# Hymba trunk in float32: the FFN's gate and up projections as seven block products with weight sums on GpSimd

## The chip, the core and the metric

The kernel runs on one core of a Trainium2 chip. TensorE (PE) multiplies matrices into PSUM, VectorE (DVE) and ScalarE (ACT) do elementwise work, GpSimd (POOL) does slow elementwise work, masks and some DMA issues, SyncE (SP) issues most of the DMAs. Each engine runs its own instructions in order and waits on semaphores of the others. The metric is the device time of one launch in microseconds (us), as a median over runs.

## What is computed

Two layers of a decoder trunk over 544 tokens (one prompt of 512, eight samples of 4), all in float32, model width 1024. Each layer is a half-step FFN, a mixer (gated DeltaNet heads and sliding-window attention), and a second half-step FFN; a norm ends the trunk. Four FFNs in all, each with a hidden width of 2816. What matters here:

```python
def _swiglu(x, w_gate, w_up, w_down):
    return (jax.nn.silu(x @ w_gate) * (x @ w_up)) @ w_down

def _layer(x, conv_buf, gdn_s, k_buf, v_buf, p):
    x = x + 0.5 * _swiglu(_rmsnorm(x, n1), g1, u1, d1)
    h = _rmsnorm(x, nm) @ w_in
    ...
    x = x + jnp.concatenate([gdn_o, swa_o], axis=-1) @ w_out
    x = x + 0.5 * _swiglu(_rmsnorm(x, n2), g2, u2, d2)
```

## The kernel before, in words

Activations are feature-major: `x` is eight tiles of 128 features by 544 tokens. A float32 product is made of three passes of a faster format (fp32r): every operand is split into a high part and a low part (what the high part leaves), and high by high, high by low and low by high are added up in PSUM. So a weight tile of 128 output columns by 1024 inputs costs 8 x 3 matmuls for each of two token halves (`HALVES`, 256 and 288 columns wide), 48 in all. The matmul is in `mm3` (L539), and `project` runs both halves.

A weight tile comes by a DMA of SP into one of three `raw` buffers. `split_w` makes `whi` on ACT (L483) and `wlo` = raw - whi on DVE (L484), each of 128 partitions by 1024 elements; `next_w` and `ahead` keep up to three loads and one split ahead of the product in progress. The plan of tiles is fixed: `HID` cuts the 22 hidden tiles of an FFN into blocks of 8, 8 and 6; in a block each hidden tile has its gate product and then its up product (a *pair*), and after the block's pairs come the eight down products over that block's hidden tiles, added into `x` (L588).

A pair's results leave PSUM on DVE, multiplied by the norm's per-token factor `rb` on the way (`scaled_evac`, L559). Then `ffn` makes the hidden value: tanh on ACT (L573), two products on DVE (L574, L575), its high part on ACT (L578) and its low part on DVE (L579).

The norm before each FFN gives the high and low parts of x times the gain (`Norm.split_half`, ACT L304 and DVE L305) and sums squares (ACT L366, POOL L372, the last of eight on DVE) while the product before it is still giving out its tiles (`Norm.tile`). At the start of the program `Norm.first` and `first_sums` do this from the token-major inputs. `later` makes the mixer's constants (masks on POOL, small gate and sink loads by POOL's DMA queue, copies of cached rows by the same queue); it is called after the first block of the first FFN, and `tc.issue_after(last_pool)` asks for its work to stand behind the last POOL instruction of the first norm (`st`, L357). A scheduler places the instructions of every engine by priority and readiness, so where such work ends up is seen in the order of each engine's instructions and in the trace.

Of the kernel before, what the change touches and what calls it, by code (L numbers as in the profile page):

```python
# [24 lines left out]
HALVES = ((0, 256), (256, 288))  # L25
EPS = 1e-6
NEG = -1e30
SLOT = 571
NSLOT = 48
# [9 lines left out]
def kernel(  # L39
# [14 lines left out]
    xt_p = ctx.enter_context(tc.tile_pool(name="xt", bufs=KD))  # L54
    raw_p = ctx.enter_context(tc.tile_pool(name="raw", bufs=3))
    w_p = ctx.enter_context(tc.tile_pool(name="w", bufs=3))
# [31 lines left out]
    # ---- streams of mixer work, woven between the dense products: a stream yields 0 after  # L88
    # each product of a batch and a number of dense products to wait for after it ----
# [5 lines left out]
    def pump(steps=1):  # L95
        """let dense time pass by one product, then streams take steps"""
# [4 lines left out]
        while steps > 0:  # L101
# [53 lines left out]
    def load_par(l, rows):  # L155
        """norm gains, conv taps and output gains, one column per 128 features"""
# [4 lines left out]
        # the rms norm's sqrt(128) and the one half of silu  # L161
# [10 lines left out]
    def mixer_constants():  # L172
# [21 lines left out]
        # second half of a pair of b-blocks by its first half, and the other way round  # L194
# [12 lines left out]
        # rows of first and of second halves  # L207
# [20 lines left out]
        # rows (sample, head, step t): 1 where j <= t, for the four leading keys  # L228
# [38 lines left out]
    # scratch: one 128 x 128 matrix per (head, chunk), spaced so that all the diagonal  # L267
    # 16-blocks lie at one stride; the inverted blocks one after another
# [12 lines left out]
    x = [slot([P, NTOK], "x") for _ in range(KD)]  # L281
    xd = dram_p.tile([KD, P, NTOK], F32, name="xd")

    class Norm:
# [3 lines left out]
        def __init__(self, nw, src=None, scale=1.0 / D, n=KD):  # L288
            self.nw, self.src, self.scale, self.n = nw, src, scale, n
# [3 lines left out]
        def split(self, k, half):  # L293
            if half == 0:
                self.xh.append(xt_p.tile([P, NTOK], F32R, tag="xh", name="xh"))
                self.xl.append(xt_p.tile([P, NTOK], F32R, tag="xl", name="xl"))
# [10 lines left out]

# [1292 lines left out]
```

## Time and profile before

| | us |
|---|---|
| median of 3 runs (2368.92 to 2373.78) | 2369.38 |
| span of the profiled execution | 2358.2 |
| PE busy in it | 2312.9 |
| DVE busy | 1238.5 |
| ACT busy | 730.6 |
| POOL busy | 267.6 |

The span runs from the first to the last instruction of the profiled execution; the 11.2 us between it and the median lie around the span. Busy times are sums of the records; a matmul's record overlaps with its neighbours', so the pace of PE is read from how many matmuls pass in a stretch, not from a record's length. The program has five kinds of stretch: the start (to 80 us), the four FFNs (about 80 to 415, 800 to 1200, 1200 to 1540 and 1935 to 2350), two mixers (about 450 to 740 and 1570 to 1890), two output projections just behind them, and the final norm inside the last FFN's last products.

### The profile page before, as it was taken

How to read it: one execution, taken by the hardware profiler on the slowest of the kernel's cores; microseconds unless marked ns; L12 is line 12 of the kernel's file. 1: busy time of each engine (PE TensorE's matmuls, PEld its weight loads, DVE VectorE, ACT ScalarE, POOL GpSimd, SP SyncE). 2: the span in 40 equal slices, each digit the busy share in tenths (PEclk: the TensorE clock that was granted, in tenths of full speed). 3: DMA queues.
4: the chain of work that ended last, by engine and by line, in shares of the span. 5: the costliest groups of instructions: out<-in, count | busy, mean ns of one | idle time of the engine just before them, and what ended most of it. 6: DMA issues, size and time to landing. Idle time of an engine off the chain costs nothing.

```text
span 2358.2 us, 41922 instructions
## 1 busy us (share of the span) xinstructions
PE 2312.9 (98%) x17683; PEld 2232.4 (95%) x17683; DVE 1238.5 (53%) x2384; ACT 730.6 (31%) x1385; POOL 267.6 (11%) x359
## 2 busy tenths in 40 slices
PE   8899999999999999999999999999999999999997
PEld 7899999998988999999999999999899799999997
DVE  5444445576567553444554343456565764444344
ACT  3222223343454321222422221244235432222122
POOL 5100000233112000000100000012231220000002
PEclk9999999998999999999999999999989899999998
DMA  5623332342124323332222333243322152233222
GB/s 127 117 83 90 90 89 90 106 120 57 48 62 142 89 83 89 90 90 87 84 87 85 89 90 90 81 131 93 75 64 64 45 160 83 89 90 90 87 77 64
DMA packets 412766, 210.37 MB, mean 89 GB/s; under 512 B 39954, under 2 KB 406866, under 8 KB 412548
## 3 DMA queue, kind: packets, MB, share of 16 engines
q1 hardware_dynamic: 410504, 204.23, 30.1%
q0 software_dynamic: 992, 2.69, 1.3%
q8 instruction: 139, 2.28, 0.4%
q10 hardware_dynamic: 1084, 0.79, 0.1%
q14 instruction: 47, 0.39, 0.0%
HBM read 192.97 MB, written 16.73 MB: 89 GB/s over the span
## 4 chain that ended last, share of the span: by engine, by line
PE 92%; DVE 3%; DMA 2%; issue 1%; POOL 1%; ACT 0%; SPq 0%; POOLq 0%; DVEq 0%; ACTq 0%
PE ps_d L539 81%; PE ps_sc L1280 1%; PE ps_sp L1273 1%; DMA sink<-in_swa_sinks_dram 1%; PE ps_s L1207 1%; PE ps_Y L929 1%; PE ps_x L1108 1%; PE ps_Z L939 1%; DMA gate<-in_gdn_a_log_dram 0%; PE ps_st L1352 0%; PE ps_av L1306 0%; PE ps_ds L1069 0%; PE ps_pt L86 0%; DVE wlo L484 0%; PE ps_qk L864 0%
## 5 line engine op out<-in xcount | busy, mean ns | idle before, releaser
L539 PE MATMUL ps_d<-xh,whi 128*128 128x256 f32 (+1 forms) x3520 | 1033.1, 294 | 14.0 <-DVE sinks L261 4.9
L539 PE MATMUL ps_d<-xl,whi 128*128 128x256 f32 (+1 forms) x3520 | 1035.8, 294 | 0.0
L539 PE MATMUL ps_d<-xh,wlo 128*128 128x256 f32 (+1 forms) x3520 | 1027.4, 292 | 0.2 <-DVE wlo L484 0.2
L483 ACT CAST whi<-raw 128x1024 fp32r<-128x1024 f32 (+1 forms) x332 | 341.3, 1028 | 1187.3 <-PE ps_d L539 781.3
L539 PEld LDWEIGHTS ps_d<-xh,whi 128*128 128x128 f32 x3520 | 669.9, 190 | 20.7 <-issue 8.9
L539 PEld LDWEIGHTS ps_d<-xh,wlo 128*128 128x128 f32 x3520 | 672.3, 191 | 6.2 <-issue 3.2
L539 PEld LDWEIGHTS ps_d<-xl,whi 128*128 128x128 f32 x3520 | 670.7, 191 | 4.7 <-issue 1.1
L484 DVE TENSOR_TENSOR wlo<-raw,whi 128x1024 fp32r<-128x1024 f32 (+1 forms) x332 | 400.2, 1206 | 117.1 <-ACT whi L483 115.9
L539 PE MATMUL ps_d<-hh,wlo 128*128 128x288 f32 (+1 forms) x1408 | 405.2, 288 | 0.0
L539 PE MATMUL ps_d<-hl,whi 128*128 128x288 f32 (+1 forms) x1408 | 404.8, 288 | 0.0
L539 PE MATMUL ps_d<-hh,whi 128*128 128x288 f32 (+1 forms) x1408 | 403.0, 289 | 0.0
L539 PEld LDWEIGHTS ps_d<-hl,whi 128*128 128x128 f32 x1408 | 266.9, 190 | 0.0
L539 PEld LDWEIGHTS ps_d<-hh,wlo 128*128 128x128 f32 x1408 | 266.8, 189 | 0.0
L539 PEld LDWEIGHTS ps_d<-hh,whi 128*128 128x128 f32 x1408 | 265.6, 190 | 0.1
L372 POOL TENSOR_TENSOR sq<-sq 128x544 f32<-128x544 f32 x40 | 60.3, 1508 | 1517.4 <-DVE wlo L484 1040.1
L588 DVE SCALAR_TENSOR_TENSOR x<-ps_d,x 128x256 f32<-128x256 f32 x192 | 83.4, 440 | 254.7 <-PE ps_d L539 254.5
L559 DVE TENSOR_TENSOR g<-ps_d,rb 128x256 f32<-128x256 f32 (+1 forms) x176 | 76.8, 437 | 237.4 <-PE ps_d L539 219.2
L559 DVE TENSOR_TENSOR u<-ps_d,rb 128x256 f32<-128x256 f32 (+1 forms) x176 | 77.5, 440 | 223.3 <-PE ps_d L539 223.3
L539 PE MATMUL ps_d<-ol,whi 128*128 128x256 f32 (+1 forms) x256 | 73.8, 291 | 0.0
L539 PE MATMUL ps_d<-oh,wlo 128*128 128x288 f32 (+1 forms) x256 | 73.6, 289 | 0.0
L539 PE MATMUL ps_d<-oh,whi 128*128 128x288 f32 (+1 forms) x256 | 72.8, 291 | 0.0
L578 ACT CAST hh<-th 128x544 fp32r<-128x544 f32 x88 | 57.1, 649 | 34.3 <-DVE th L575 34.3
(399 smaller groups left out, 2080.5 us busy)
## 6 DMA issues: line engine op xcount, KB each, us to landing
raw<-in_ffn_w_gate_dram SPq DMA_DIRECT2D x88, 512.0 KB
raw<-in_ffn_w_up_dram SPq DMA_DIRECT2D x88, 512.0 KB
raw<-in_ffn_w_down_dram SPq DMA_DIRECT2D x64, 512.0 KB
raw<-in_w_in_dram SPq DMA_DIRECT2D x36, 512.0 KB
raw<-in_ffn_w_down_dram SPq DMA_DIRECT2D x32, 384.0 KB
S<-in_state_gdn_dram SPq DMA_DIRECT2D x32, 256.0 KB
xd<-x SPq DMA_DIRECT2D x16, 272.0 KB
x<-xd SPq DMA_DIRECT2D x16, 272.0 KB
```

The lines of the kernel that those rows point to most:

```text
L372: eng.tensor_tensor(out=self.sq, in0=self.sq, in1=s2, op=ALU.add)
L483: act.copy(out=hi[:, 0:kn], in_=v)
L484: dve.tensor_tensor(out=lo[:, 0:kn], in0=v, in1=hi.bitcast(F32)[:, 0:kn], op=ALU.subtract)
L539: pe.matmul(ps, a[:, k], b, start=(k == 0 and a is hi and b is rh), stop=(k == kn - 1 and a is lo))
L559: when(norm, lambda: dve.tensor_tensor(out=dst[:, o:o + n], in0=ps, in1=norm.rb[:, o:o + n], op=ALU.mult))
L578: act.copy(out=a, in_=th)
L588: dve.scalar_tensor_tensor(out=xv, in0=ps, scalar=0.25, in1=xv, op0=ALU.mult, op1=ALU.add)
L929: pe.matmul(ps[:, q], NM[q // 4][:, q % 4], T[:, q], start=True, stop=True)
L939: pe.matmul(ps[:, q], Tt[q // 4][:, q % 4], Y[:, q], start=True, stop=True)
L1108: pe.matmul(ps[:, :, r0:r0 + 4], ss[s // 4][:, s % 4], kqs[:, :, 32 * h + r0:32 * h + r0 + 4], start=True, stop=True)
L1207: pe.matmul(ps, kd[32 * h:32 * h + 32], um[i][32 * h:32 * h + 32], start=True, stop=True)
L1273: pe.matmul(ps[:, hh], sq[hh][gp, qs], kfe[gp, (n - 1) * P:n * P], start=True, stop=True)
```

## The change

**Seven products.** The two k halves (even and odd k tiles) and the two token halves of a pair's gate and up products make a 2 x 2 block product, which needs seven block products in Strassen's scheme instead of eight. One such product is over four k tiles and 272 tokens (`T0`, `T1`), 12 matmuls (`mm7`), so a pair has 84 matmuls of 272 columns where it had 96 of 256 and 288. Three weight blocks of a product are plain (b11, b21, b22), four are sums `t1`, `nt2`, `t3`, `t4`, made on POOL in `queue_pair` from the two raw tiles, 128 x 512 elements each. All seven are split (`split_part`, half tiles of 128 x 512).

**Activations.** `Norm.blocks` makes seven blocks of activations (three plain, four sums s1, ns2, s3, s4, the third on POOL) for each two k tiles, each with a high and a low part.

**Results.** `gate_up` leaves PSUM seven times: three by a copy on ACT, three by an addition to that copy on DVE, and one on DVE with the factor `rb`. The factor for the other three quarters of gate and up is now a POOL multiplication in place: half of g (272 columns), all of u (544).

**Around it.** `HID` is now 6, 6, 6 and 4; raw tiles have four buffers, half tiles of high and low parts six each, `AHEAD` is 3; a hidden value's parts (`parts`) are made in the next pair; and `later` has lost its `issue_after`.

```diff
+HT = NTOK // 2
+T0, T1 = slice(0, HT), slice(HT, NTOK)
...
+NW = 6
+AHEAD = 3
...
-    raw_p = ctx.enter_context(tc.tile_pool(name="raw", bufs=3))
-    w_p = ctx.enter_context(tc.tile_pool(name="w", bufs=3))
+    raw_p = ctx.enter_context(tc.tile_pool(name="raw", bufs=4))
+    w_p = ctx.enter_context(tc.tile_pool(name="w", bufs=NW))
...
+        def blocks(self, i):
...
+            part("a11", a[:, T0], v)
+            part("a12", b[:, T0], w)
+            act.activation(out=s1, in_=b[:, T1], func=ACTF.Copy, scale=w)
+            dve.scalar_tensor_tensor(out=s1, in0=a[:, T1], scalar=v, in1=s1, op0=ALU.mult, op1=ALU.add)
+            dve.scalar_tensor_tensor(out=ns2, in0=a[:, T0], scalar=v, in1=s1, op0=ALU.mult, op1=ALU.subtract)
+            pool.tensor_tensor(out=s3, in0=a[:, T0], in1=a[:, T1], op=ALU.subtract)
+            dve.scalar_tensor_tensor(out=s4, in0=b[:, T0], scalar=w, in1=ns2, op0=ALU.mult, op1=ALU.add)
+            part("s1", s1, None)
+            part("ns2", ns2, None)
+            part("s3", s3, v)
+            part("s4", s4, None)
+            part("a22", b[:, T1], w)
...
+        def total(n, in0, in1, op):
+            T[n] = slot([P, 4, P], "wt")
+            pool.tensor_tensor(out=T[n], in0=in0, in1=in1, op=op)
+
+        def third():
+            total("t3", b22, b12, ALU.subtract)
+            total("t4", b21, T["nt2"], ALU.add)
+            return split_part(T["nt2"])
+
+        total("t1", b12, b11, ALU.subtract)
+        total("nt2", T["t1"], b22, ALU.subtract)
...
-    HID = ((0, 8), (8, 8), (16, 6))
+    HID = ((0, 6), (6, 6), (12, 6), (18, 4))
...
+        def plus(out, ps):
+            dve.tensor_tensor(out=out, in0=ps, in1=out, op=ALU.add)
+
+        def scale(t, part):
+            pool.tensor_tensor(out=t[:, part], in0=t[:, part], in1=norm.rb[:, part], op=ALU.mult)
...
+            mm7(pb, next_half(), bk["a11"], start=True)
+            act.copy(out=g[:, T0], in_=pb)
+            mm7(pa, next_half(), bk["a12"], start=True)
+            plus(g[:, T0], pa)
+            scale(g, T0)
...
+            mm7(pb, next_half(), bk["ns2"])
+            act.copy(out=u[:, T0], in_=pb)
+            mm7(pd, next_half(), bk["s1"], start=True)
+            act.copy(out=u[:, T1], in_=pd)
+            mm7(pb, next_half(), bk["s3"])
+            plus(u[:, T1], pb)
+            mm7(pd, next_half(), bk["s4"])
+            plus(u[:, T0], pd)
+        scale(u, slice(0, NTOK))
+        mm7(pb, next_half(), bk["a22"])
+        dve.tensor_tensor(out=g[:, T1], in0=pb, in1=norm.rb[:, T1], op=ALU.mult)
...
-        with tc.issue_after(last_pool):
-            for l in range(depth):
-                par.append(load_par(l, load_par_rows(l, nc.gpsimd)))
...
+        for l in range(depth):
+            par.append(load_par(l, load_par_rows(l, nc.gpsimd)))
```

DVE in the middle of an FFN's block, one pair of before (`wlo` is a split of a whole weight tile, `g` and `u` are evacuations):

```order
L484 TENSOR_TENSOR wlo<-raw,whi 128x1024
L559 TENSOR_TENSOR u<-ps_d,rb 128x256
L574 SCALAR_TENSOR_TENSOR th<-th,g 128x544
L559 TENSOR_TENSOR u<-ps_d,rb 128x288
L575 TENSOR_TENSOR th<-th,u 128x544
L484 TENSOR_TENSOR wlo<-raw,whi 128x1024
L579 TENSOR_TENSOR hl<-th,hh 128x544
L559 TENSOR_TENSOR g<-ps_d,rb 128x256
L559 TENSOR_TENSOR g<-ps_d,rb 128x288
```

DVE at the same place of the changed kernel, 12 of the 14 rows of one pair (`wt` is a weight sum, `raw_562` the up tile of the next pair, `ps_b`, `ps_a` and `ps_d` the three PSUM tiles):

```order
L523 TENSOR_TENSOR wlo_874<-wt_781,whi_873 128x512
L708 TENSOR_TENSOR g_658<-ps_b_660,rb_420 128x272
L523 TENSOR_TENSOR wlo_891<-raw_562,whi_890 128x512
L720 SCALAR_TENSOR_TENSOR th_800<-th_800,g_658 128x544
L664 TENSOR_TENSOR g_804<-ps_a_807,g_804 128x272
L523 TENSOR_TENSOR wlo_908<-raw_562,whi_907 128x512
L721 TENSOR_TENSOR th_800<-th_800,u_659 128x544
L523 TENSOR_TENSOR wlo_930<-wt_832,whi_929 128x512
L727 TENSOR_TENSOR hl_849<-th_800,hh_848 128x544
L523 TENSOR_TENSOR wlo_956<-wt_830,whi_955 128x512
L523 TENSOR_TENSOR wlo_973<-wt_925,whi_972 128x512
L664 TENSOR_TENSOR u_805<-ps_b_806,u_805 128x272
```

Two splits of 1024 have become seven of 512, spread between the evacuations, and the splits run up to a pair ahead of the products.

POOL in the same stretch of the changed kernel, one pair (before, it has no instruction there):

```order
L535 TENSOR_TENSOR wt_684<-raw_560,raw_445 128x512
L535 TENSOR_TENSOR wt_686<-wt_684,raw_560 128x512
L667 TENSOR_TENSOR g_658<-g_658,rb_420 128x272
L535 TENSOR_TENSOR wt_779<-raw_560 128x512
L535 TENSOR_TENSOR wt_781<-raw_445,wt_686 128x512
L667 TENSOR_TENSOR u_659<-u_659,rb_420 128x544
```

The two scalings stand between sums of the next pair, each behind the evacuation that it scales.

POOL at the start of the program, before: the norm's factor `st`, then the mixer's constants.

```order
L344 TENSOR_TENSOR xtok<-xtok 128x512
L352 TENSOR_TENSOR xtok<-xtok 128x512
L381 MEMSET st 128x5
L357 TENSOR_TENSOR st<-st,mhalf 128x5
L174 MEMSET upper 128x128
L177 MEMSET lower 128x128
```

POOL at the start of the changed kernel, the place where `st` stands now (`xs` is s3 of the third k pair of the first norm):

```order
L252 DMA gate_1785<-in_gdn_dt_bias_dram 128x4x4
L135 AFFINE_SELECT selba<-selba 128x8
L256 DMA gate_1785<-in_gdn_dt_bias_dram 128x1x1
L135 AFFINE_SELECT eye_1764<-eye_1764 128x256
L393 TENSOR_TENSOR st<-st,mhalf 128x5
L339 TENSOR_TENSOR xs<-x 128x272
L260 DMA sink_1786<-in_swa_sinks_dram 128x8
L1706 DMA out_dram<-in_cache_swa_k_dram 8x15872
```

The constants and the gate and sink loads now stand ahead of `st`; behind the last row come three more copies of cached rows, then s3 of the fourth k pair and the first weight sums.

## Rows read from the trace of the kernel before

**Rows 1.** The page, parts 1 and 4: busy times, and the chain by line.

```profile
PE 2312.9 (98%) x17683; PEld 2232.4 (95%) x17683; DVE 1238.5 (53%) x2384; ACT 730.6 (31%) x1385; POOL 267.6 (11%) x359
...
PE 92%; DVE 3%; DMA 2%; issue 1%; POOL 1%; ACT 0%; SPq 0%; POOLq 0%; DVEq 0%; ACTq 0%
```

**Rows 2.** Busy time by stretch of time: busy us and instructions by engine, granted clock, DMA.

```profile
core 0: us, PE busy (x) PEld busy (x) DVE busy (x) ACT busy (x) POOL busy (x), PEclk, DMA share, GB/s
17.00:78.00 61.00, 53.27 (x400) 50.50 (x400) 29.22 (x64) 20.00 (x38) 29.52 (x78) 1.00 0.62 72
...
800.00:1200.00 400.00, 399.79 (x3183) 399.37 (x3182) 190.22 (x289) 107.89 (x137) 10.13 (x8) 1.00 0.30 87
```

**Rows 3.** Chain that ended last, the longest piece of an FFN: start, us, what.

```profile
795.74 392.44 PE ps_d L539 x3122
```

**Rows 4.** Timeline of DVE, one pair: start, us, operation, idle before and its releaser.

```profile
841.08 0.42 DVE L559 TENSOR_TENSOR u<-ps_d,rb 128x256 f32<-128x256 f32 x1 [0.61 <-PE ps_d L539]
841.42 0.71 DVE L574 SCALAR_TENSOR_TENSOR th<-th,g 128x544 f32<-128x544 f32 x1
...
845.42 1.22 DVE L484 TENSOR_TENSOR wlo<-raw,whi 128x1024 fp32r<-128x1024 f32 x1
846.55 0.72 DVE L579 TENSOR_TENSOR hl<-th,hh 128x544 fp32r<-128x544 f32 x1
847.19 0.41 DVE L559 TENSOR_TENSOR g<-ps_d,rb 128x256 f32<-128x256 f32 x1
...
853.13 0.42 DVE L559 TENSOR_TENSOR u<-ps_d,rb 128x256 f32<-128x256 f32 x1 [0.61 <-PE ps_d L539]
```

**Rows 5.** Groups of instructions by shape: count, busy us, mean ns, idle before.

```profile
L573 ACT ACTIVATE th<-g 128x544 f32<-128x544 f32 x88 | 57.4, 652 | 9.2 <-DVE g L559 9.1
L578 ACT CAST hh<-th 128x544 fp32r<-128x544 f32 x88 | 57.1, 649 | 34.3 <-DVE th L575 34.3
L352 POOL TENSOR_TENSOR xtok<-xtok 128x512 f32<-128x512 f32 x2 | 2.5, 1272 | 0.1
```

**Rows 6.** Timelines of POOL and DVE, output projection, 764 to 784 us.

```profile
764.92 1.37 POOL L372 TENSOR_TENSOR sq<-sq 128x544 f32<-128x544 f32 x1 [4.67 <-ACT sq L366]
```

**Rows 7.** The same stretch, DVE beside that POOL instruction and without one.

```profile
764.97 1.64 DVE L305 SCALAR_TENSOR_TENSOR xl<-x,par,xh 128x288 fp32r<-128x288 f32 x1
...
783.08 0.52 DVE L305 SCALAR_TENSOR_TENSOR xl<-x,par,xh 128x288 fp32r<-128x288 f32 x1
783.51 0.72 DVE L372 TENSOR_TENSOR sq<-sq 128x544 f32<-128x544 f32 x1
```

**Rows 8.** Timelines of DVE and POOL at 564 to 568 us (first mixer), short windows.

```profile
565.31 0.69 DVE L890 TENSOR_TENSOR Tt<-T,bd 128x512 f32<-128x512 f32 x1
...
565.92 1.76 DVE L890 TENSOR_TENSOR Tt<-T,bd 128x512 f32<-128x512 f32 x1
...
565.42 1.72 POOL L935 TENSOR_TENSOR NM<-NT,pmt 128x512 f32<-128x512 f32 x1
...
567.10 1.74 POOL L935 TENSOR_TENSOR NM<-NT,pmt 128x512 f32<-128x512 f32 x1
```

**Rows 9.** Timelines at 569 to 573 us: DVE, a PSUM operand and a split; POOL.

```profile
570.07 0.67 DVE L884 TENSOR_TENSOR VI<-ps_v,ik 128x512 f32<-128x512 f32 x1
570.67 2.18 DVE L484 TENSOR_TENSOR wlo<-raw,whi 128x1024 fp32r<-128x1024 f32 x1
...
570.38 1.39 POOL L758 TENSOR_TENSOR cacc<-cacc,cacb 128x568 f32<-128x568 f32 x1
```

**Rows 10.** Chain that ended last, the start of the program.

```profile
30.54 1.19 POOL st L357
...
48.36 11.27 DMA gate<-in_gdn_a_log_dram
59.91 18.14 DMA sink<-in_swa_sinks_dram
...
80.63 98.84 PE ps_d L539 x768
```

**Rows 11.** Work of L539 alone before 81 us: PE, its loads, clock, DMA.

```profile
0.00:81.00 81.00, 54.01 (x386) 50.62 (x387) 0.98 0.67 114
```

More of the change, by code (lines that the diff above doesn't have):

```diff
@@ L361, in tile @@
             xk = x[k] if self.src is None else self.src[k]
-            if self.nw is not None:
+            if self.seven:
+                if k % 2:
+                    self.blocks(k // 2)
+            elif self.nw is not None:
                 self.split(k, 0)
@@ L476, in load_raw, with split_part, queue_pair, take @@
         return raw
-    def split_w(raw, kn=KD):
-        hi = w_p.tile([P, KD, P], F32R, tag="whi", name="whi")
-        lo = w_p.tile([P, KD, P], F32R, tag="wlo", name="wlo")
-        v = raw[:, 0:kn]
-        act.copy(out=hi[:, 0:kn], in_=v)
-        dve.tensor_tensor(out=lo[:, 0:kn], in0=v, in1=hi.bitcast(F32)[:, 0:kn], op=ALU.subtract)
-        return hi, lo
+    def split_part(v):
+        hi, lo = (w_p.tile([P, 4, P], F32R, tag=n, name=n) for n in ("whi", "wlo"))
+        hi, lo = hi[:, 0:v.shape[1]], lo[:, 0:v.shape[1]]
+        act.copy(out=hi, in_=v)
+        dve.tensor_tensor(out=lo, in0=v, in1=hi.bitcast(F32), op=ALU.subtract)
+        return hi, lo
+    def queue_pair(wg, wu):
+        b11, b21 = wg[:, 0::2], wg[:, 1::2]
+        b12, b22 = wu[:, 0::2], wu[:, 1::2]
+        T = {}
+        def total(n, in0, in1, op):
[7 more added lines that the diff above has]
+        total("nt2", T["t1"], b22, ALU.subtract)
+        jobs.extend([lambda: split_part(b11), lambda: split_part(b21), third, lambda: split_part(T["t1"]),
+                     lambda: split_part(T["t3"]), lambda: split_part(b22), lambda: split_part(T["t4"])])
+    def take():
+        if not raws:
+            return False
+        if raws[0][1] == "pair":
+            if len(raws) < 2:
+                return False
+            (wg, _), (wu, _) = raws.pop(0), raws.pop(0)
+            queue_pair(wg, wu)
+        else:
+            raw, kn = raws.pop(0)
+            for k in range(0, kn, 4):
+                jobs.append(lambda v=raw[:, k:min(k + 4, kn)]: split_part(v))
+        return True
     def ahead(loads, splits):
@@ L490, in ahead, with next_half @@
             raws.append((load_raw(pieces), kn))
-        while raws and len(split) < splits:
-            split.append(split_w(*raws.pop(0)))
-    def next_w(here=0):
-        ahead(1, 1)
+        while len(split) < splits and (jobs or take()):
+            split.append(jobs.pop(0)())
+        if len(jobs) < 3:
+            take()
+    def next_half(here=AHEAD):
+        ahead(2, 1)
         w = split.pop(0)
@@ L507, in plan_ffn @@
             for j in range(h0, h0 + kn):
[L508 to L509 removed]
+                for w in (wg, wu):
+                    plan.append((cols(w, j * P)[0], "pair"))
             for q in range(KD):
@@ L563, in ffn @@
+    tail = []
     def ffn(norm, nxt, after=None, before_last=None):
-        xt = (norm.xh, norm.xl)
         for h0, kn in HID:
@@ L1537 @@
     act.copy(out=ones[:, 0:1], in_=ones[:, 0:1])
-    norm = Norm(None)
+    norm = Norm(None, seven=True)
     norm.first(rows, 0, (0, 1))
```

130 lines of the change are left out of this document (91 added, 39 removed).

## The prediction

> **What bounds the kernel now.** I read the page's busy times first, then its chain of waits: PE is busy for 98% of the span and 92% of the chain is PE [rows 1]. The table by stretch says the same of a single FFN: between 800 and 1200 us, 399.79 us of PE at full clock, while DVE is busy for 190.22 us and POOL for 10.13 [rows 2]. The chain gives the pace there: 392.44 us for 3122 matmuls, 0.1257 us each [rows 3], whether 256 or 288 columns wide, so 0.126 for 272. A pair of gate and up products is 96 matmuls or 12.07 us; DVE's timeline repeats after 853.13 - 841.08 = 12.05 us [rows 4]. In that period DVE is idle for half of the time. So before, PE alone sets the end, and matmuls taken away would be a gain as long as DVE and POOL keep up. That is the question.
>
> **What is removed.** 12 of 96 matmuls in each of 88 pairs: 1056 x 0.1257 = 133 us. A pair could take 84 x 0.1257 = 10.56 us.
>
> **What is added to a pair.** DVE had two splits of 1024 and four evacuations; now it has seven splits of 512, the same three operations of 544 for the hidden value, and four evacuations of 272. From start to start, a 1024 split takes 1.13 us (845.42 to 846.55) and an operation of 544 takes 0.64 (846.55 to 847.19) [rows 4]; two DVE operations of 512 in a row, 565.31 and 565.92, are 0.61 apart [rows 8], I take 0.60. So 7 x 0.60 + 3 x 0.65 = 6.15 us of operations that read two SBUF tiles, and 4 x 0.36 = 1.45 of evacuations (0.34 for 256 columns, 841.08 to 841.42 [rows 4]). 7.6 us alone would fit into 10.56. ACT has 7 high parts, 3 copies, tanh and a high part at 0.65 [rows 5], by these some 6 us, and fits too. POOL, which had nothing there, gets four sums of 512 (1.27 us for one with two full operands [rows 5]) and scalings of 272 and 544 (0.69 and 1.37, from the 544 sum of [rows 6]): 7.1 us, which would fit as well.
>
> **But DVE and POOL don't run side by side.** The split of an activation takes 0.52 us on its own at 783.08, and 1.64 at 764.97 [rows 7], just behind the start of a POOL sum at 764.92 [rows 6]: 1.12 us longer, nearly the POOL operation's 1.37. A weight split that meets a POOL operation takes 2.18 us instead of 1.22 ([rows 9], [rows 4]). Where both want to run all the time they take turns: POOL's two start 1.68 us apart, and DVE's operation of 512 takes 1.76 instead of 0.69 [rows 8], that is 0.60 for DVE and 1.08 for POOL, one after the other. An operation with one operand in PSUM isn't held up: 0.67 us at 570.07, while POOL runs from 570.38 [rows 9].
>
> The Trainium skill ("SBUF — State Buffer", section "Who interferes with whom") states this as a rule: a DVE instruction with two SBUF inputs contends with a GpSimd instruction that reads SBUF, for an exclusive lock, and one with at most one SBUF input does not. The rows above agree on both halves of it. The rule speaks against this change, whose POOL work is all of the contending kind; without it the sum would be that of the second rival below.
>
> So a pair's work on the shared path is 6.15 for DVE and for POOL 4 x 1.08 + 0.58 + 1.17 (0.85 of an operation's length, as 1.17 from 764.92 to the end of the wait was of 1.37) = 6.07 us: 12.2 us, more than 10.56 and about the 12.07 of before. DVE's own line is longer: 6.15 + 1.45 + 6.07 = 13.7 us if no evacuation falls into POOL's turns, 12.2 if all do. POOL holds the path for about 46% of the time, so by chance 0.46 x 1.45 = 0.67 us are hidden: 13.0. The order has one split (0.60) between a pair's last evacuation and the operation that needs its tanh (0.65 on ACT, and two handovers): 0.2 us of waiting. I take **13.2 us** for a pair, with 12.2 and 14.1 as ends (the upper from the third rival). PE then runs 10.56 of 13.2 us. I expect no lower clock from that: between 17 and 78 us PE issued 400 matmuls in 61 us, 0.82 of its pace, at clock 1.00 [rows 2].
>
> **A block.** The sums and six of the splits of a block's first pair stand under the down products before it, where DVE has little to do: 6 x 0.60 + 4.32, less 0.4 that would have been hidden anyway, 7.5 us. A block's first product has to end before its first evacuation: 1.5 us. Six pairs: 6 x 13.2 - 7.5 + 1.5 = 73.2 us against 72.4 before. Four pairs: 52.8 - 6.0 = 46.8, and its end is bare: from the last product, evacuation, tanh, two operations, high part and low part take about 3.9 us, and the first down tile holds back only one k tile of four, 18 matmuls or 2.3 us of cover (30 and 3.8 us for blocks of six): 1.5 us more, 48.3 against 48.3. An FFN is 3 x 0.8 = 2.4 us longer, four of them **+10 us**. The whole removal of 133 us goes into the wait for splits and sums.
>
> **The start.** Before, 386 of L539's matmuls were issued by 81 us [rows 11], 48.5 us of work, so 32.5 us were lost. The order puts the masks and the loads of gates and sinks ahead of st and of POOL's sums, and DVE's and ACT's work on those loads ahead of the last activation blocks, without which no first product ends; PE has 18 matmuls (2.3 us) until then. The masks took from 31.73 to 48.36 [rows 10], so about 16.6 us earlier the loads go out near 32. If they land at once, PE goes on at 37, a loss of 37 - 2.3 = 34.7 us, 2 more than before; if they need the 29.7 us that both took (48.36 to 78.05 [rows 10]), it is 62, 27 more. Four raw buffers are soon full and quiet the DMA queues, so I take a little under the middle: **+13**.
>
> **Ends of FFNs.** Where the seven blocks of activations are made behind the last down products (layer 0's second FFN), two down tiles are 48 matmuls, 6.0 us. For them DVE has about ten operations of 272 at 0.41 (0.43 for 288, 783.08 to 783.51 [rows 7]), two splits and four evacuations, 6.75, and POOL s3 and two sums of squares, 2.9: 9.65 us. Four times 3.65 less some cover: **+12**. Before a mixer and at the last norm the down tiles are only 3.0 us long (4.5 before) and DVE and POOL need 3.3: **+5** and **+4**. At the output projections the tiles are 6.03 us and DVE has the blocks and the next pair's splits: **+5** for both, nothing if they fit.
>
> **Sum.** 10 + 13 + 12 + 5 + 4 + 5 = 49 us on the span of 2358.2, so 2407; with the 11.2 us around it as before, **2418 us**.
>
> **Rivals.**
> 1. *Faster: the turns interlock.* All evacuations fall into POOL's turns, and a pair is the 12.2 us of the shared path. For: POOL's queue has work most of the time, splits run up to a pair ahead, so nobody needs to be on time. Against: POOL waits for two evacuations in each pair (the scalings). Six pairs: 73.2 - 7.9 + 1.5 = 66.8; four: 43.9; 21 us less for an FFN. 2369 - 85 + 39 = 2323, or 2302 with the other terms at their low ends. It decides at 12.64 us for a pair, where 88 x 0.56 makes up the 49.
> 2. *PE still bounds.* The two engines hold each other up less than in the rows (a pair of 10.56): 2369 - 133 + 39 = 2275. Against: every meeting of theirs in the rows shows the full wait.
> 3. *Whole instructions and more waits.* Each takes its full length in turn: 7 x 0.69 + 3 x 0.72 for DVE, 4 x 1.27 + 0.69 + 1.37 for POOL: 14.1 us even with all evacuations hidden. 88 x 0.9 = 79 more: 2497. The same comes from POOL waiting idle for an evacuation while DVE waits for a sum. For: both engines run strictly in order, and each waits for the other twice in a pair. Against: the turns of 1.68 us [rows 8] are shorter than the two lengths together. The Trainium skill (same page and section) has it that the first to issue holds the pair of ports for the whole instruction; by that rule this rival is the case, and the trace agrees only in part: 1.12 of 1.37 us.
> 4. *The start alone:* loads that land as late as before add 14 to the forecast: 2432.
>
> **Chances.** Forecast (12.7 to 13.8 us for a pair, with the fourth rival, 2374 to 2471) 0.50; first rival 0.16; second 0.04; third 0.27; the rest, 0.03, falls near no change. The range leaves out the second rival, the low end of the first and a tail of the third: 2320 to 2510. A difference of 0.2%, 4.7 us, is about what can be told from none: faster 0.20, within it 0.04, slower 0.76.
>
> **What would show it.** In the steady part of an FFN the same DVE row should come back after 13.2 us (10.6 would prove the second rival, 12.2 the first, 14 the third). The POOL sums should be recorded at 1.6 to 1.9 us and DVE's splits of 512 at about 1.2 on average instead of 0.69; PE's idle time should be put down to DVE's `wlo`. PE should be busy for some 80% of an FFN at full clock. In the first 60 us PE should stand still after 18 matmuls until the sinks have landed. I am wrong if splits keep their 0.69 beside POOL sums, or if the FFNs are faster and the ends between them eat the gain.

## The result, and the profile after

The changed kernel takes 2501.87 us (median of 4 runs, 2496.24 to 2510.13) against 2369.15 (2366.90 to 2373.78): the ratio is 1.0565, 95% interval 1.0529 to 1.0602. The forecast was 2418 us, in a range that holds the measured time; the change was forecast at +49 us and is +133. The third rival's 2497 is close to the time, but as will be seen not for the third rival's reason, so that the range holds it is luck.

The page of the changed kernel, parts 1 and 4 (compare [rows 1]):

```profile
span 2505.7 us, 43432 instructions
...
PE 2290.5 (91%) x16627; PEld 2161.4 (86%) x16627; DVE 1847.3 (74%) x3172; ACT 1053.7 (42%) x2341; POOL 1079.5 (43%) x903
...
PE 66%; DVE 21%; issue 7%; ACT 3%; POOL 2%; DMA 1%; DVEq 0%; ACTq 0%; SPq 0%; POOLq 0%
```

1056 matmuls are gone (17683 to 16627), POOL's busy time has gone from 267.6 to 1079.5 us and DVE's from 1238.5 to 1847.3, and PE, 92% of the chain before, is 66% of it now, with DVE at 21%.

One steady pair, DVE and then POOL (start, us, operation; one pair of before is [rows 4]), with the `L708` row of the next pair:

```profile
1010.98 0.43 DVE L664 TENSOR_TENSOR u<-ps_b,u 128x272 f32<-128x272 f32 x1
1011.33 0.68 DVE L523 TENSOR_TENSOR wlo<-raw,whi 128x512 fp32r<-128x512 f32 x1
1011.92 0.43 DVE L664 TENSOR_TENSOR u<-ps_d,u 128x272 f32<-128x272 f32 x1
1012.28 0.68 DVE L523 TENSOR_TENSOR wlo<-wt,whi 128x512 fp32r<-128x512 f32 x1
1013.27 0.44 DVE L708 TENSOR_TENSOR g<-ps_b,rb 128x272 f32<-128x272 f32 x1 [0.31 <-PE ps_b L652]
1013.80 0.93 DVE L523 TENSOR_TENSOR wlo<-raw,whi 128x512 fp32r<-128x512 f32 x1
1014.65 1.81 DVE L720 SCALAR_TENSOR_TENSOR th<-th,g 128x544 f32<-128x544 f32 x1
1016.38 0.43 DVE L664 TENSOR_TENSOR g<-ps_a,g 128x272 f32<-128x272 f32 x1
1016.73 1.43 DVE L523 TENSOR_TENSOR wlo<-raw,whi 128x512 fp32r<-128x512 f32 x1
1018.08 1.29 DVE L721 TENSOR_TENSOR th<-th,u 128x544 f32<-128x544 f32 x1
1019.29 1.76 DVE L523 TENSOR_TENSOR wlo<-wt,whi 128x512 fp32r<-128x512 f32 x1
1020.97 1.81 DVE L727 TENSOR_TENSOR hl<-th,hh 128x544 fp32r<-128x544 f32 x1
...
1026.21 0.44 DVE L708 TENSOR_TENSOR g<-ps_b,rb 128x272 f32<-128x272 f32 x1 [0.32 <-PE ps_b L652]
...
1012.43 1.74 POOL L667 TENSOR_TENSOR u<-u,rb 128x544 f32<-128x544 f32 x1 [3.17 <-DVE u L664]
1014.14 1.74 POOL L535 TENSOR_TENSOR wt<-raw 128x512 f32<-128x512 f32 x1
1015.96 1.66 POOL L535 TENSOR_TENSOR wt<-wt,raw 128x512 f32<-128x512 f32 x1
1017.57 1.22 POOL L667 TENSOR_TENSOR g<-g,rb 128x272 f32<-128x272 f32 x1
1018.75 1.76 POOL L535 TENSOR_TENSOR wt<-raw 128x512 f32<-128x512 f32 x1
1020.46 1.74 POOL L535 TENSOR_TENSOR wt<-raw,wt 128x512 f32<-128x512 f32 x1
```

The same split of 512 takes 0.68 us at 1011.33, while POOL waits 3.17 us for an evacuation, and 1.43 or 1.76 us while POOL works. An evacuation keeps its 0.43 us throughout, also at 1016.38, in the middle of a POOL sum. The `L708` row comes back every 12.9 us. By stretch (us and instructions by engine, granted clock; before was [rows 2]), two pairs:

```profile
1002.00:1028.00 26.00, 22.96 (x171) 21.62 (x171) 25.19 (x29) 12.69 (x25) 18.62 (x12) 1.00 0.22 63
```

DVE is busy or held up for 25.19 of 26 us; PE issues 171 matmuls where 207 would fit, at full clock. DVE hardly waits for anyone (0.31 us in the pair shown): its line is full, with operations that POOL makes longer.

Where the 147.5 us of the two profiled executions (2358.2 and 2505.7) went, by stretches cut at the first product of each stage. By the medians it is 133: the changed kernel's profiled execution took 2507.43 us for a span of 2505.7, and wherever both times of an execution are known some 2 us lie around the span. So of the 11.2 us that the prediction puts around the span of before, about 9 are that this execution was faster than the median.

| stretch | before, us | after, us | difference | forecast |
|---|---|---|---|---|
| start and first FFN | 432.7 | 477.8 | +45.1 | +18 |
| two mixers | 287.3 + 291.8 | 303.3 + 304.7 | +28.9 | 0 |
| two output projections | 60.8 + 62.4 | 60.8 + 69.4 | +7.0 | +5 |
| layer 0's second and layer 1's first FFN | 802.0 | 847.8 | +45.8 | +19 |
| last FFN and the end | 421.3 | 441.9 | +20.6 | +6 |

So nearly 100 us of these are missing in the forecast, and the mixers, which the change doesn't touch, hold 29 of them.

### The profile page after: what moved, and what is told of

Read it like the earlier page. It is cut to its first block, busy times and chain, and to the rows that moved or that the text cites. A ratio compares the mean times of both kernels' runs of the same rounds, so it can differ in the third digit from the quotient of the medians.

```text
span 2505.7 us, 43432 instructions
## 1 busy us (share of the span) xinstructions
PE 2290.5 (91%) x16627; PEld 2161.4 (86%) x16627; DVE 1847.3 (74%) x3172; ACT 1053.7 (42%) x2341; POOL 1079.5 (43%) x903
## 4 chain that ended last, share of the span: by engine, by line
PE 66%; DVE 21%; issue 7%; ACT 3%; POOL 2%; DMA 1%; DVEq 0%; ACTq 0%; SPq 0%; POOLq 0%
PE ps_d L622 35%; PE ps_b L652 13%; DVE wlo L523 9%; PE ps_d L652 5%; DVE hl L727 3%; PE ps_a L652 2%; DVE th L721 2%; ACT whi L522 2%; PE ps_sc L1432 1%; DVE xhl L328 1%; DVE u L664 1%; DVE th L720 1%; DMA gate<-in_gdn_a_log_dram 1%; PE ps_s L1359 1%; PE ps_Y L1081 1%
## 5 line engine op out<-in xcount | busy, mean ns | idle before, releaser
L652 PE MATMUL ps_b<-xhl,whi 128*128 128x272 f32 x2816 | 579.0, 301 | 116.6 <-ACT u L699 43.7
L523 DVE TENSOR_TENSOR wlo<-raw,whi 128x512 fp32r<-128x512 f32 x608 | 511.0, 843 | 162.5 <-ACT whi L522 142.8
L522 ACT CAST whi<-raw 128x512 fp32r<-128x512 f32 x608 | 354.7, 586 | 618.8 <-PE ps_d L622 341.9
L652 PEld LDWEIGHTS ps_b<-xhl,whi 128*128 128x128 f32 x2816 | 457.1, 195 | 145.5 <-ACT u L699 52.8
L652 PE MATMUL ps_b<-xhl,wlo 128*128 128x272 f32 x1408 | 418.0, 297 | 9.2 <-DVE wlo L523 9.2
L523 DVE TENSOR_TENSOR wlo<-wt,whi 128x512 fp32r<-128x512 f32 x352 | 344.6, 998 | 61.8 <-ACT whi L522 58.3
L535 POOL TENSOR_TENSOR wt<-raw 128x512 f32<-128x512 f32 x176 | 275.0, 1563 | 224.2 <-DMA raw<-in_ffn_w_up_dram 224.2
L652 PE MATMUL ps_d<-xhl,whi 128*128 128x272 f32 x1408 | 276.9, 291 | 10.9 <-ACT whi L522 6.0
L652 PEld LDWEIGHTS ps_b<-xhl,wlo 128*128 128x128 f32 x1408 | 274.3, 195 | 12.1 <-DVE wlo L523 11.8
L622 PE MATMUL ps_d<-xl,whi 128*128 128x256 f32 (+1 forms) x704 | 226.5, 322 | 0.0
```

The source lines that it names most:

```text
L522: act.copy(out=hi, in_=v)
L523: dve.tensor_tensor(out=lo, in0=v, in1=hi.bitcast(F32), op=ALU.subtract)
L535: pool.tensor_tensor(out=T[n], in0=in0, in1=in1, op=op)
L622: pe.matmul(ps, a[:, k % 4], b, start=(k == 0 and a is hi and b is rh), stop=(k == kn - 1 and a is lo))
L652: pe.matmul(ps, a[:, k], b, start=start and k == 0 and i == 0, stop=k == 3 and i == 2, skip_group_check=not start)
```

## Experiments

Times are medians; each ratio is to the kernel before on the same chip (2369.15, 2360.79, 2364.99 and 2365.71 us there). Stretches are of one profiled execution each. A *block* is the time from one large down stretch to the next, for blocks of six pairs: 110.7 or 112.0 us in the changed kernel (112.3 once), 6 x (12.07 + 6.03) = 108.6 by the pace of before, and 99.6 if PE never waited.

| run | us | ratio (95%) | block of six | mixers |
|---|---|---|---|---|
| before | 2369.15 | 1 | 108.6 | 287.3, 291.8 |
| changed kernel | 2501.87 | 1.0565 (1.0529 to 1.0602) | 110.7 to 112.3 | 303.3, 304.7 |
| e1_no_pool | 2328.64 | 0.9862 (0.9815 to 0.991) | 101.2 | 298.2, 292.0 |
| e2_dve | 2359.09 | 0.9994 (0.9965 to 1.0023) | 102.1 | 303.8, 293.0 |
| e3_constants | 2509.94 | 1.061 (1.0541 to 1.068) | 110.7 to 112.3 | 303.8, 304.5 |
| e4_half | 2375.12 | 1.0044 (1.0016 to 1.0073) | as before | 296.3, 297.4 |
| e5_late | 2521.85 | 1.0662 (1.0614 to 1.0709) | 110.7 to 112.1, the second 157.6 | 300.7, 304.5 |
| e6_whole | 2573.69 | 1.089 (1.0857 to 1.0924) | 116.9 to 118.2 | 290.9, 288.6 |
| e7_best | 2450.46 | 1.0371 (1.0331 to 1.0412) | 110.1 to 111.6, the second 125.9 | 309.2, 306.0 |
| e8_blocks | 2455.63 | 1.0393 (1.0326 to 1.046) | 110.7 to 112.2 | 304.9, 306.8 |
| e9_dve_late | 2357.90 | 0.9966 (0.9937 to 0.9996) | 102.1, the second 120.3 | 299.8, 304.6 |
| e10_norm_dve | 2361.40 | 0.997 (0.9941 to 0.9999) | 102.0, the second 119.9 | 304.7, 303.6 |
| e11_scale | 2379.17 | 1.0064 (1.0026 to 1.0102) | 104.4 | 288.9, 297.8 |

### Is it the turns of DVE and POOL? e1_no_pool

```diff
-            T[n] = slot([P, 4, P], "wt")
-            pool.tensor_tensor(out=T[n], in0=in0, in1=in1, op=op)
+            T[n] = in0
...
-            pool.tensor_tensor(out=t[:, part], in0=t[:, part], in1=norm.rb[:, part], op=ALU.mult)
+            pass
```

> The changed kernel without POOL's work in a pair: raw weight blocks stand in for the four weight sums, and the two scalings by the norm's factor are left out (the FFN's share in x is also made tiny, so that values stay finite). DVE, ACT and PE keep all their instructions. Theory (DVE and POOL hold each other up): a steady pair falls from 12.93 us to PE's own 10.6, about 2.3 us for each of some 70 steady pairs and a little at the FFNs' ends, so 2502 - 170 = about 2330 us. Rival (the order of waits between PE, ACT and DVE is too long, for instance the copies on ACT that release a PSUM tile): a pair stays above 12 us and the time above 2440.

Measured 2328.64 us. A stretch of the length of two pairs of the changed kernel, all matmuls and all DVE and ACT work in place:

```profile
1030.00:1056.00 26.00, 26.00 (x209) 26.00 (x208) 21.48 (x36) 16.72 (x32) 0.00 (x0) 1.00 0.37 108
```

209 matmuls in 26 us are PE's own pace of 0.125 us. Without POOL's six operations in a pair nothing else holds PE up: neither ACT's copies nor the order of waits. The theory's 2330 is met, the rival falls. This run takes away POOL's turns and the waits for POOL's results together; that it is the turns is seen in DVE's rows above, longer beside POOL and without waits.

### The same work on DVE: e2_dve, e11_scale

```diff
-            pool.tensor_tensor(out=T[n], in0=in0, in1=in1, op=op)
+            dve.tensor_tensor(out=T[n], in0=in0, in1=in1, op=op)
...
-            pool.tensor_tensor(out=t[:, part], in0=t[:, part], in1=norm.rb[:, part], op=ALU.mult)
+            dve.tensor_tensor(out=t[:, part], in0=t[:, part], in1=norm.rb[:, part], op=ALU.mult)
```

> The changed kernel with the four weight sums and the two scalings on DVE instead of POOL. Theory (the two engines take turns anyway, and POOL's turn of 1.08 us costs more than DVE's own 0.60): DVE's line is 7.6 + 4 x 0.60 + 0.33 + 0.65 = 11.0 us for a pair, so a pair of 11.0 to 11.4 instead of 12.93, some 1.7 x 70 = 120 us less: about 2380 us. Rival (DVE's strict order makes it worse, since sums now stand ahead of evacuations): 13 us or more for a pair, 2500 or more.

e11_scale has the first of these two edits alone.

> The changed kernel with the weight sums on DVE and the two scalings left on POOL. Theory (turns add up): DVE's 7.6 + 2.4 = 10.0 us and POOL's two turns of 0.58 and 1.17, less what falls beside evacuations: 11.4 to 11.75 us for a pair, between the 11.0 of all on DVE and the 12.93 of all on POOL; blocks of six near 104 to 105 us, total near 2385. Rival (only a queue full of POOL work delays DVE, two operations find gaps): 11.0 and 2359.

Measured 2359.09 and 2379.17 us. The blocks of 102.1 and 104.4 us, less 36.2 for the down products, are 11.0 and 11.4 us for a pair on average, against 12.4 to 12.6 in the changed kernel. DVE with all the work on it, two pairs:

```profile
1040.00:1066.00 26.00, 25.80 (x200) 25.17 (x199) 25.98 (x48) 14.56 (x29) 0.00 (x0) 1.00 0.29 83
```

DVE is busy for 25.98 of 26 us with 48 instructions, where it was busy for 25.19 with 29 beside POOL: the time that it is held up was counted as busy time there. The group of splits from raw tiles shows the price of one neighbour (us, mean ns), first of the changed kernel, then of e11_scale, then of e2_dve:

```profile
L523 DVE TENSOR_TENSOR wlo<-raw,whi 128x512 fp32r<-128x512 f32 x512 | 453.9, 888 | 157.2 <-ACT whi L522 137.5 <-PE ps_d L622 8.4 <-PE ps_cn L89 1.5
```

```profile
L523 DVE TENSOR_TENSOR wlo<-raw,whi 128x512 fp32r<-128x512 f32 x512 | 403.8, 790 | 102.8 <-ACT whi L522 90.8 <-PE ps_cn L89 1.5 <-DMA raw<-in_w_out_dram 0.3
```

```profile
L523 DVE TENSOR_TENSOR wlo<-raw,whi 128x512 fp32r<-128x512 f32 x512 | 359.8, 704 | 116.1 <-ACT whi L522 105.3 <-PE ps_d L622 4.2 <-PE ps_cn L89 1.5
```

Two scalings on POOL cost a pair 0.4 us, four sums on POOL a further 1.0 to 1.3. Between steady pairs, by the `L708` row, it is 10.9 to 11.0 us in e2_dve, 11.34 in e11_scale and 12.93 in the changed kernel. The faster place for a POOL operation is the engine that it holds up.

### The start: e3_constants, e5_late

e3_constants gives `later` its `issue_after(last_pool)` back:

```diff
+        with tc.issue_after(last_pool):
```

> The changed kernel with the mixer's constants held behind the first norm's last POOL instruction again, as before the change. Theory (the start is late because the first sums on POOL and the first activation blocks on DVE stand behind gate and sink loads): the order changes only in the first 80 us; the activation blocks come earlier, the first block's end (first down product, 143.8 us now) 10 to 20 us earlier, about 2485 us. Rival (the first weight sums stand behind the constants either way, so nothing is won): 2502, or up to 10 more.

Measured 2509.94 us, no change, and the first large down stretch starts at 149.1 us instead of 143.9: in this order PE has a single wait of 30.7 us, up to 65.6, where the changed kernel has waits of 11.9 us and less. e5_late holds the constants until the first block is done:

```diff
+        tick = sm("tick", (P, 1))
+        behind = pool.tensor_tensor(out=tick, in0=x[KD - 1][:, 0:1], in1=x[KD - 1][:, 1:2], op=ALU.add).ins
+        with tc.issue_after(behind):
+            constants()
```

> The changed kernel with the mixer's constants and small loads held behind a POOL instruction that reads the last result of the first block's down products, so that nothing of them stands at the start any more. Theory (the late start is theirs: the last activation blocks stand behind the sink loads on DVE, which land at about 62 us): PE's long stop at 51 to 63 us goes, and the first block's large down stretch (154.3 us now) starts 15 to 25 us earlier. But on POOL the constants (25 us and the loads' waits) now stand in a row ahead of the second block's weight sums, so that block gets longer by about as much (112.3 us now) and the total stays near 2500. Rival (the start is bound by DVE's and POOL's own new work): the first down stretch stays at 150 or later.

The first large down stretch starts at 123.2 us, 20.7 earlier than the changed kernel's 143.9 (the expectation's 154.3 and 51 to 63 us, and the 141.6 in that of e9_dve_late, count from a zero 10.5 us ahead of the rows'); the second block takes 157.6 us instead of 112.3, and the total is 2521.85. So 21 us of the late start are the constants' and their loads', and they cost more where POOL is needed in the second block. PE's steady work begins here, in the changed kernel and then in e5_late:

```profile
66.90 0.82 PE L652 MATMUL ps_d<-xhl,whi 128*128 128x272 f32 x2 [5.97 <-ACT whi L522]
```

```profile
45.71 0.82 PE L652 MATMUL ps_d<-xhl,whi 128*128 128x272 f32 x2 [2.79 <-ACT whi L522]
```

The start of the changed kernel, DVE and then POOL, shows how:

```profile
51.24 2.59 DVE L267 TENSOR_SCALAR nea<-nea 128x17 f32<-128x17 f32 x1 [5.01 <-ACT nea L266]
...
60.04 1.43 DVE L337 SCALAR_TENSOR_TENSOR xs<-x,n1t,xs 128x272 f32<-128x272 f32 x1
...
62.54 1.58 DVE L338 SCALAR_TENSOR_TENSOR xs<-x,n1t,xs 128x272 f32<-128x272 f32 x1
...
52.50 1.28 POOL L535 TENSOR_TENSOR wt<-raw 128x512 f32<-128x512 f32 x1
53.87 1.49 POOL L535 TENSOR_TENSOR wt<-wt,raw 128x512 f32<-128x512 f32 x1
```

DVE stands until the gates have landed at about 51 us (`nea`), and when it may go on with the last activation blocks, POOL makes its first eight weight sums in a row, and most of DVE's operations take one of POOL's turns: 1.43 and 1.58 us for 272 elements. The sums are the smaller part: without them (e1_no_pool) PE has issued 148 of these matmuls by 81 us instead of 118, which is 3.8 us.

### The mixers: e4_half, e6_whole, e7_best

e4_half is the kernel before, with split tiles of 128 x 512 and six buffers of them.

```diff
-    w_p = ctx.enter_context(tc.tile_pool(name="w", bufs=3))
+    w_p = ctx.enter_context(tc.tile_pool(name="w", bufs=6))
...
     def split_w(raw, kn=KD):
...
-        hi = w_p.tile([P, KD, P], F32R, tag="whi", name="whi")
-        lo = w_p.tile([P, KD, P], F32R, tag="wlo", name="wlo")
...
+        return [split_part(raw[:, k:min(k + 4, kn)]) for k in range(0, kn, 4)]
```

> The kernel before with weight tiles split in halves of 128 x 512 and six buffers of half tiles, as the change has it, and nothing else. The changed kernel's mixers are 16 and 13 us longer (287.3 to 303.3 us, 291.8 to 304.7), which nothing in the prediction covers. Theory (half tiles make the mixer's order longer): mixers near 303 us and about 2369 + 29 = 2398 us. Rival (it is the slots, which the norm's parts now share with the mixer, or what the scheduler makes of them): mixers as before, 2369.

Mixers of 296.3 and 297.4 us: 9 and 6 longer, 0.4% of the time. e6_whole is the changed kernel with whole tiles wherever it isn't gate or up; a pair's half tiles share buffers of whole ones there.

```diff
-            for k in range(0, kn, 4):
-                jobs.append(lambda v=raw[:, k:min(k + 4, kn)]: split_part(v))
+            jobs.append(lambda v=raw[:, 0:kn]: split_whole(v))
```

> The changed kernel with the weight tiles of the mixers, output projections and down products split whole (128 x 1024) again; halves only for gate and up. Theory (half tiles, which cost the kernel before 9 and 6 us in its mixers, are a part of the mixers' 16 and 13 us): mixers at about 293 and 297 us instead of 303.3 and 304.7, and some 15 us off the total: 2487. Rival (what the norm's parts do to the shared slots, or the order the scheduler finds): mixers stay at 303 and 305, 2502.

The mixers are back at 290.9 and 288.6, as the theory has it. But the blocks take 117 to 118 us, probably since two half tiles now free their buffer together and the splits can't run as far ahead; so the total is 2573.69, a loss that I hadn't expected. e7_best puts e2_dve, e6_whole and e5_late together.

> A version meant to be faster than both: weight sums and scalings on DVE (2359 us so far, FFN blocks of 102 us where the changed kernel has 112), whole splits outside gate and up, and the constants held behind the first block. Theory (three separate costs that add up): 2359 less 10 to 15 at the start and less 10 to 18 in the mixers, 2330 to 2340, about 1% under the kernel before. Rival (the mixers' length comes from the scheduler's order and moves either way, the start is bound by DVE): 2350 to 2365, no difference to before.

2450.46 us: blocks of 110 to 112 (102.1 in e2_dve), by the same reasoning, and mixers of 309.2 and 306.0 with whole tiles. That undoes what e6_whole seemed to say: it isn't the size of the splits.

The granted clock says what it is. PE in a stretch of the first mixer, in the changed kernel and then in the kernel before:

```profile
580.00:621.00 41.00, 41.00 (x160) 36.43 (x160) 13.74 (x30) 8.71 (x22) 10.93 (x15) 0.50 0.16 34
```

```profile
539.00:550.00 11.00, 11.00 (x36) 8.06 (x35) 2.60 (x7) 1.91 (x3) 2.19 (x4) 0.53 0.49 97
```

The clock falls to its lower level (1.2 GHz, 0.50) here in both; PE had issued 41 and 48 matmuls in 8 us shortly before (572 to 580 and 529 to 537), where 64 would fit. Before, it comes back within 11 us. In the changed kernel it stays there for 41 us, with PE never idle in the records; dense products come three at a time between a mixer's small ones, at 0.28 us each (0.125 at the full clock). The chain in that stretch:

```profile
605.78 0.83 PE ps_d L622 x3
606.61 0.24 PE ps_Y L1081 x2
```

Over 26 mixers (two each of 13 kernels) the mean clock and the length go together: 0.91 to 0.94 with 287.3 to 293.0 us, 0.89 and 0.90 with 296.3 to 300.7, 0.87 to 0.89 with 303.3 to 309.2. From 0.94 to 0.87 in 300 us are 42 us more at half speed, 21 us of work lost, nearly the whole difference. Between the kernel before and the changed one it is a part: by the traces' clock records TensorE stood at the lower level for 44 and 55 us before, 68 and 72 after, which is, at half speed, 12 and 9 us of the 16 and 13, and in e4_half (61 and 65 us) 8 and 5 of the 9 and 6. The other 4 us in each mixer of the changed kernel stay open.

PE's order in the mixers differs from the kernel before in each of the kernels (the scheduler weaves dense and small products anew when anything ahead is changed), but the order doesn't settle the clock: nearly the same one has given 304.7 and 293.0 (changed kernel and e2_dve, second mixer) and 303.3 and 288.9 (changed kernel and e11_scale, first). Even one program varies: over 29 executions of the kernel before, on one chip, the mean clock of the whole goes from 0.963 to 0.980 and the time with it from 2384.95 to 2350.76 us. The changed kernel's four, at 0.951 to 0.958, are all below that, so a lower clock does come with the change; a mixer's length in one profile is still that of one execution. What tips the clock in one mixer and not in another stays open.

### The end of an FFN: e8_blocks

```diff
...
+            for name, of in (("s1", "a12"), ("ns2", "a11"), ("s3", "a11"), ("s4", "a22")):
+                self.blk[name].append(self.blk[of][-1])
```

> The changed kernel without the four activation sums s1, ns2, s3, s4 and their parts: the parts of a plain block stand in for them (and the FFN's share in x is made tiny, so that values stay finite). All matmuls stay. Theory (the end of layer 0's second FFN is bound by DVE, which makes seven blocks for each two k tiles there): from the last block's large down stretch to the next FFN's first one 123 us become 100 to 105, and the second output projection (69.4 us) goes back to 62; the start gets some 10 us shorter. Rival (the wait there is for the norm's factor, or for the first weight sums): 120 us stay.

Measured 2455.63 us. From large down stretch to large down stretch across the end of layer 0's second FFN: 107.2 us instead of 123.0; the second output projection 63.0 instead of 69.4; the first down stretch 8 us earlier. The theory holds for the FFN's end, nearly: 107.2 is a little above its 105, and what remains above the 100.9 us that would be no loss (25.6 of down products, six old pairs, 2.9 that it lost before) is 6. The changed kernel's chain there, and the stretch behind it:

```profile
1271.10 1.44 DVE xs L337
...
1272.56 1.39 DVE xs L338
1273.95 1.42 DVE xhl L325
1275.37 1.43 DVE xs L340
```

```profile
1270.00:1285.00 15.00, 8.56 (x34) 7.26 (x34) 12.50 (x18) 6.25 (x14) 9.70 (x8) 0.50 0.24 70
```

The last k pair's blocks are made after the last down product, operation by operation, the rows shown with one of POOL's turns in each (1.4 us for 272 elements, 0.41 alone), and PE, with 34 matmuls in 15 us, falls to half clock. From 1234.8 to 1357.7 us it stands at the lower level for 20.5 us, in e8_blocks for 3.4 and before not at all, so that up to 10 of the 22 us lost there are the clock's.

For the output projections the theory doesn't hold. The two of the changed kernel, the second and then the first, and the second of e8_blocks:

```profile
1994.30:2063.80 69.50, 66.34 (x425) 58.91 (x426) 54.62 (x112) 28.94 (x69) 23.75 (x19) 0.88 0.39 117
781.10:841.90 60.80, 59.20 (x426) 53.51 (x426) 53.90 (x118) 28.47 (x68) 25.91 (x20) 1.00 0.47 136
```

```profile
1973.00:2036.00 63.00, 60.56 (x425) 54.89 (x425) 46.33 (x97) 23.15 (x53) 22.70 (x19) 0.97 0.47 138
```

The first makes the same blocks and takes the 60.8 us of before, at full clock; the second's 69.4 stand at a clock of 0.88, 17 us at the lower level, half of which is the whole excess. In all 26 output projections the length less half of the time at the lower level is 59 to 61 us. What the blocks cost there comes after: from the first product behind a projection to the large down stretch it is 85.5 and 89.0 us, and 79.9 and 82.2 in e8_blocks, some 3 us of each difference being the clock.

### A version faster than both? e9_dve_late, e10_norm_dve

e9_dve_late is e2_dve with the constants of e5_late; POOL has nothing else to do where they stand.

> Weight sums and scalings on DVE, half tiles everywhere as in the changed kernel, and the mixer's constants held behind the first block's down products, where POOL now has nothing else to do. Theory (the start's 20 us, found when the constants were moved in the changed kernel, and the blocks of 102 us add up): first large down stretch at 122 to 128 us instead of 141.6, 15 to 18 us off 2359, about 2343, unless the mixers' clock takes it back: they have been between 287 and 309 us long in the kernels so far, by how long TensorE's granted clock stood at its lower level. Rival (the constants collide on DVE and POOL in the second block as they did with sums on POOL): the second block gets longer by 10 or more and 2359 stays.

e10_norm_dve also has s3 and the sums of squares of the seven-block norms on DVE.

```diff
-            pool.tensor_tensor(out=s3, in0=a[:, T0], in1=a[:, T1], op=ALU.subtract)
+            dve.tensor_tensor(out=s3, in0=a[:, T0], in1=a[:, T1], op=ALU.subtract)
...
-                eng = dve if self.seen == self.n - 1 else pool
+                eng = dve if self.seven or self.seen == self.n - 1 else pool
```

> The same, and in the norms that make seven blocks also s3 and the sums of squares on DVE. Theory (two engines that take turns are slower than one, here too): for two k tiles DVE has 1.7 us more and is spared 2.9 us of POOL's turns, so the end of layer 0's second FFN (112 us from large down stretch to large down stretch with sums on DVE) gets 4 to 6 us shorter and the output projections 0 to 3 each: about 2336. Rival (the wait there is a chain of single operations, not the sum of the engines' work): no difference to the run before.

2357.90 and 2361.40 us. In the first, the first large down stretch starts at 109.5 us instead of e2_dve's 131.0, and the second block takes 120.3 instead of 102.2: the rival is right, the constants cost 18 of their 21 us again there, as the waits of ACT and DVE in that stretch show (us in total, times, longest):

```profile
ACT nea L266 <- DMA gate<-in_gdn_a_log_dram: 14.5, 2, 8.3
```

```profile
DVE nea L267 <- ACT nea L266: 8.8, 2, 5.7
...
DVE pick L263 <- DMA sink<-in_swa_sinks_dram: 4.9, 2, 2.9
```

What stands behind a waiting operation on its engine, ACT's copies out of PSUM among it, waits too: PE waits 6.59 us in one piece for ACT's copy of u, up to 181.1. In e10_norm_dve, the end of the FFN takes 110.7 us instead of 112.0, so the theory's 4 to 6 us aren't there and the sum of the engines' work isn't what bounds it any more; that a chain of single operations does, as the rival has it, no run tests. Both are 0.3% under the kernel before, with an interval that just leaves out no difference; the removal of 133 us of matmuls is worth no more here, with mixers of 300 to 305 us.

## Why the prediction was wrong

**The mechanism was right and is shown.** A pair was put at 13.2 us, by turns of 1.08 us for a POOL operation; it takes 12.93. e1_no_pool (10.56), e2_dve (11.0), e11_scale (11.34) and the changed kernel give the ladder that the sum of turns gives. Most of the rows named beforehand are there: splits at 0.68 and 1.4 to 1.8 us, POOL sums at 1.54 to 1.72 us on average, the pair back after 12.9 us, PE at 0.83 of its pace and at full clock. Two are not: the splits of raw tiles take 0.89 us and those of weight sums 1.00 on average instead of 1.2, since those that fall into POOL's waits keep their 0.68, and PE's idle time is put down to ACT's copy of u and DVE's evacuations (7.5 and 9.1 us from 927 to 1234 us), which stand behind the splits, and to `wlo` itself with 2.1 only. The first rival (12.2) was not reached, most likely because POOL waits for evacuations (3.17 us in the pair shown); the second (10.56) and the third (14.1) don't fit a pair of 12.93, though the time came out near the third's 2497. The row that the prediction takes for an evacuation beside POOL (0.67 us at 570.07) began ahead of POOL's operation and shows little; the 0.43 us at 1016.38, inside a sum from 1015.96 to 1017.62, show it. The rule that the Trainium skill gives ("SBUF — State Buffer", sections "SBUF: two separate sides" and "Who interferes with whom") is borne out in its main point, evacuations from PSUM beside POOL's sums included; that a turn lasts the whole instruction is too much by the rows, 1.08 to 1.17 us of 1.27 to 1.37.

**What failed are terms around it,** that is the four steps that follow and one that wasn't there.

*The block: 73.2 us, measured 74.5 to 75.8* (110.7 to 112.0 less 36.2). The 7.5 us of credit for sums and splits under the down products were too much: 6 x 12.93 + 1.5 = 79.1, so 3 to 5 were had. From 1038 to 1090 us ACT's high parts wait for down products:

```profile
ACT whi L522 <- PE ps_d L622: 21.3, 10, 3.3
```

So the splits can't run ahead there, and the six half-tile buffers are the likely bound; e6_whole, with less room ahead, has blocks 6 us longer. Over the trace the blocks of six are some 17 us. The blocks of four take 50.0 us (84.7 less 34.7 of down products) where the sum had 48.3: 7 for four.

*The start: +13, measured +33.* The first down products stand at 140.1 us (143.9 less 3.8 for the 30 of them that are issued ahead of the last pair's end), where the kernel before, with six pairs instead of its eight ahead of them, would have had them at 131.0 - 24.1 = 106.9. The step "PE goes on between 37 and 62 us" ended the sum at the landing of the loads. PE's steady work began at 66.9 with 25 products issued, 63.8 us lost, where the sum had 32.5 + 13. e5_late gives 21 us of it to the constants; without them it still loses 42.7 us by 45.7, 10 more than before, where the sum's lower end had 2: behind the landing there are a k pair's blocks and the first splits, and POOL's sums hold them up by some 4 us.

*The end of layer 0's second FFN: +12, measured +22* (122.9 against 100.9). The step counted the engines' work for four k pairs against four times two down tiles. It left out that the last k pair's blocks come after the last down tile, in a chain with a turn in most links, and that PE loses its clock in it. e8_blocks gives 16 of the 22 back. The ends ahead of the mixers and of the program came out as forecast: 3.0 and 2.6 us against +5 for both, 3.4 against +4.

*The mixers: not in the sum, measured +29.* I took work that the change doesn't touch to be as long as before. Its pace is the granted clock's, and some 21 of the 29 are that. The clock was looked for only in the FFNs ("I expect no lower clock"), where it holds in the steady pairs: 1.00. Over the whole profiled execution TensorE stood at its lower level for 239 us (mean clock 0.952), and for 122 before (0.974): 117 more, which is at most 58 us of the 147.

*Output projections: +5, measured +7*, all in the second and all of it the clock, so the nearness of the two numbers is luck. The blocks made under the projections cost 6 and 10 us in the first block behind each (85.5 and 89.0 us less 3.8, against 99.5 less 24.1), where the sum had 0.8.

Of the 98 us missing between the two profiled executions, the mixers are 29, the start 19, the blocks of six 17, the output projections with the blocks behind them 17, the FFN's end 9 and the blocks of four 7.

**The constants.** That their new place costs time was in the sum, at the wrong size. e3_constants and e9_dve_late show that no place is free: with `issue_after` back nothing is won, and behind the first block 18 of 21 us return.

## What to carry to other kernels

A DVE operation with two SBUF operands and a POOL operation that reads SBUF are one queue: add their times, and put POOL's elementwise work on DVE if it is in a steady loop with DVE (0.60 us there for 1.08 of turns, in this kernel). When PE is relieved, sum the work of the engines behind it not only for the loop but for each joint, and there as a chain: the last item's operations one after the other, each with a neighbour's turn in it. And where a woven stage runs at a granted clock of 0.9, count some 20 us in 300 as open for any change ahead of it, touched or not, and set the clock of each stage beside its time before a difference is given to the work in it.

## What the runs showed of the hardware

A DVE operation with one SBUF operand was held up too: `nea`, a TENSOR_SCALAR of 128 x 17, takes 2.59 us at 51.24 while POOL goes through memsets, s3 and the first weight sum nearly without a break, and 0.17 us for the same operation in the kernel before (59.97). The Trainium skill ("SBUF — State Buffer", section "Who interferes with whom") says that `tensor_scalar` can enter a two-port mode in which it contends with GpSimd; this row agrees, one case only.

And a granted clock at its lower level can stay for 41 us without a moment of idle PE in the records (580 to 621 us), with 160 matmuls issued in that time.
